# Gated values and attention keys and values as one product of 512 columns, with a new table of delays, in a two-layer hybrid decoder trunk

## The chip, the cores and the metric

The kernel runs on one core of a Trainium2 chip. The core's engines work side by side: TensorE (PE, matrix products), VectorE (DVE), ScalarE (ACT), GpSimd (POOL) and SyncE (SP, which here only issues transfers); 16 DMA engines move data between the large memory outside and the core. Each engine works through its own list in order, and semaphores make one wait for another. The metric is the device time of one execution in microseconds (us).

## What is computed

Two layers over 1024 tokens of 1024 features. In each, one projection of the normalised input is split into three groups of heads, whose gated outputs are put side by side and projected back:

```python
mod = c_act @ w_mod + b_mod
shift, scale, gate = jnp.split(mod[:, None, :], 3, axis=-1)
h = rms_norm(x, pre_gain) * (1.0 + scale) + shift
proj = h @ w_in
(aq, ak, av, ag, rq, rk, rv, rg, gq, gk, gv, gg, ga) = jnp.split(proj, IN_SPLITS, axis=-1)
...
a_out = sliding_window_attention(aq, ak, av, sinks) * jax.nn.silu(ag)
...
r_out = rms_norm(r).reshape(B, S, RET_W) * jax.nn.silu(rg)
...
g = gated_linear_attention(gq..., gk..., gv..., log_a)
g_out = rms_norm(g, gla_norm_gain).reshape(B, S, GLA_W) * jax.nn.silu(gg)
y = jnp.concatenate([a_out, r_out, g_out], axis=-1) @ w_out
return x + gate * rms_norm(y, post_gain)
```

The columns that matter here are `gv` (256: values of the gated linear attention, GLA), and `ak` and `av` (128 each: keys and values of the windowed attention, called kv in the kernel).

## The kernel before

**Products.** Every large product is done in a split form: an operand is a high and a low part in the fp32r type, and three passes (high·high, low·high, high·low) over eight slices of 128 features make 24 matmuls for a tile of 128 tokens. `accum` (L577) issues them. `project` (L586) makes 256 columns of one weight, `project_2` (L599) makes 512 columns out of two weights at once (already used for rk and rv), and `project_T` makes a transposed product. Results land in PSUM, in eight banks of 512 columns: three are called `mm` and hold the projections, five are called `aux` and hold all smaller products.

**Order.** The order of PE's instructions is written by the program itself, since the trunk is recorded under `manual_schedule` for PE; the other engines' instructions are put in order by the framework. The main line issues projections. Everything else is a generator, called a job: it issues some instructions, then yields a delay, or the name of a flag that it needs, and goes on once a clock kept by the program has passed that time. The clock `clk` adds a fixed cost for every matmul that is issued (`mult`, L169). `pump` (called every 7 matmuls of 256 columns or every 4 of 512) lets jobs go on that are due. So a delay decides how many projection matmuls stand on PE between a job's steps; it is no wait on the chip. The delays are the table `L`, read by `lat(key, l)`, which takes the entry `key@1` in layer 1 where there is one. Names in it: `gc1` to `gc6` are the GLA core, `mod1` to `mod6` the modulation, `pre1` the pre-norm, `fin1` and `lay1` the end of a layer, `kv1` and `kv2` the attention keys, `gl1` the GLA gate.

**Input stage of a layer.** After gates (gg, rg) and retention (rq, rk, rv), the projections of gq and gk (`do_gqk`, four of 512 columns), gv (`do_gv`, eight tiles of 256) and kv (`do_kv`, eight tiles of 256) follow. Weights come by DMA in pieces, are split by ACT, DVE (L501) and POOL (L501) into high and low parts in an arena, and `load(l, name)` starts that for the next weight.

**GLA core.** After two tiles of gv a job `gla_core` (L1236) is made, four in a layer, two tiles (cores of 128 tokens, index c) in each. DVE prepares decayed queries and keys (L1244, L1245), PE makes 28 small score matmuls per c into four aux banks (L1269, L1275), ACT (L1278) and DVE (L1279) copy them out, and after the delay `gc3` the next c follows. Then PE multiplies with the running state `stG` (L1291), and DVE updates the state (L1300, L1301); the delay `gc5` sets when the next tile may use it. On DVE also stands the modulation of the next layer: L318 multiplies a piece of modulation weights (buffer `ms`, three buffers) as soon as it has landed, 60 times in all, and L642 normalises in `pre` (L630's function), the first step of the next layer.

**The last product.** In the last layer, `last_output` adds partial results: ACT copies a bank into `kept` (L1518), DVE adds (L1522), ACT squares (L1526).

The lines that carry the three passes:

```python
for a, b in PASSES:
    for k in ks:
        mult(dst, lhs_of(a, k), rhs_of(b, k), q == 0 and ks[0] == 0, ...)
        q += 1
        if q % (CHUNK if len(dst.shape) == 2 else CHUNK // 2 + 1) == 0:
            pump()
```

Of the kernel before, what the change touches and what calls it, by code (L numbers as in the profile page):

```python
# [22 lines left out]
NP_ = NT // 2  # L23
# [68 lines left out]
def trunk(ctx: ExitStack, tc: tile.TileContext, ins, cst, out):  # L92
# [37 lines left out]
    def mm():  # L130
        return ps.tile([P, 512], F32, tag="mm", name=nm("mm"), bufs=MMB)
# [259 lines left out]
    def tables_T():  # L391

        tbs = []
        for i in range(2):
            yield L["tt1"] if i == 0 else L["tt2"]
            pt = aux()
# [61 lines left out]
    def used(l, name):  # L458
        await_flag(("w", l, name))
        return unit(l, name)  # L460
# [14 lines left out]
    def load(l, name, first=None):  # L475
        if l >= DEPTH:
            return
        src = w_out[l] if name[0] == "o" else w_in[l]
        sv = src[ORDER[name]]

        def issue(kc):
            st = stage().rearrange("p (k n) -> p k n", k=2)
            dma("lw", st, sv[:, 2 * kc:2 * kc + 2, :])
            return (st,)

        def conv(kc, st):
            wt = unit(l, name)
            hi, lo = (wt[:, a, 2 * kc:2 * kc + 2, 0:256] for a in range(2))
            if name[0] == "o" and kc == 3:
                A.activation(hi, st, AF.Copy, scale=gnc[:, l:l + 1])  # L490
                V.scalar_tensor_tensor(lo, st, gnc[:, l:l + 1], f(hi), ALU.mult, ALU.subtract)
            else:
                if first:
                    A.activation(hi, st, AF.Copy)
                else:
                    copy(f"whi{kc}", hi, st)
                if first:
                    e = G if first == "AG" and kc in (1, 2) else V
                else:
                    e = G if name[0] == "o" and kc == 2 else eng(f"wlo{kc}")  # L500
                e.tensor_tensor(lo, st, f(hi), ALU.subtract)  # L501
            if kc == 3:
                if name == "gg" and not first:
                    gt = wt[:, :, :, 256:272]
                    st = t1()
                    sg = st[:, 0:128].rearrange("p (k n) -> p k n", k=KT)
                    nc.sync.dma_start(sg, w_ga[l])
                    A.activation(gt[:, 0], sg, AF.Copy)
                    V.tensor_tensor(gt[:, 1], sg, f(gt[:, 0]), ALU.subtract)
                flag(("w", l, name))  # L510

        if first:
            return Paced(issue, conv)
        for kc in range(KT // 2):
            request(l, 1, lambda kc=kc: issue(kc), lambda st, kc=kc: conv(kc, st))
# [410 lines left out]
    kv = {}  # L926
# [707 lines left out]
    def layer(l):  # L1634
# [39 lines left out]
        for t in range(NT):  # L1674
            pm = mm()
# [25 lines left out]
            if hf and kk:  # L1701
                load(l, "aq0")

        def do_gv(p):
            for t in (2 * p, 2 * p + 1):
                pm = mm()
                project(pm[:, 0:256], l, t, used(l, "gv"))
                vs[t] = t1()
                copy("gv", vs[t], pm[:, 0:256])
                if t % 2:  # L1710
                    job(gla_core(l, p, qks[p], (vs[t - 1], vs[t])))
                pump()
            if p == NP_ - 1:
                load(l, "aq1")

        def do_kv(p):
            if p == 0:
                new_kv()
            for t in (2 * p, 2 * p + 1):
                pk = mm()  # L1720
                project(pk[:, 0:256], l, t, used(l, "kv"))
                job(attn_kv(l, t, pk))
                pump()

        do_gqk(0, 0)
        do_gqk(0, 1)
        do_gv(0)
        do_gqk(1, 0)
        do_gv(1)
        do_gqk(1, 1)  # L1730
        do_gv(2)
        do_kv(0)
        do_gv(3)
        for p in range(1, NP_):
            do_kv(p)
        load(l, "ag0")
        job(attn_run(l))
        mx = {}
# [108 lines left out]
L = {"tt6": 5.81, "sw1": 0.0, "ld1": 1.44, "ld2": 1.76, "ld1@1": 1.47, "ld2@1": 1.28, "swW00": 7.11, "swT1": 0.0, "swW11": 1.11, "swW10": 5.83, "tt1": 18.44, "tt2": 2.17, "tt3": 0.28, "tt4": 6.38, "rq1": 14.03, "pf3": 2.74, "pf4@2": 4.29, "pf4@3": 6.52, "pf5": 0.72, "mod1": 2.49, "mod2": 2.57, "mod3": 8.78, "mod4": 9.72, "mod5": 2.35, "mod6": 9.18, "pre1": 4.11, "kv1": 4.46, "kv2": 4.0, "aq1": 5.98, "aq7": 6.05, "ag1": 3.7, "aq2": 2.37, "aq6": 4.8, "aq3": 10.37, "aq4": 6.89, "aq5": 4.91, "hn1": 8.92, "hn2": 2.9, "gz1": 15.13, "gz2": 13.15, "gl1": 2.41, "gd3": 16.85, "gc1": 0.0, "gc2": 1.89, "gc3": 2.35, "gc4": 0.0, "gc6": 0.0, "gc5": 0.87, "rc1": 3.27, "rc2": 3.14, "rc3": 6.62, "rc4": 6.04, "fin1": 6.53, "lay1": 3.11, "gc4@1": 0.0, "mod2@1": 3.98, "mod3@1": 12.28, "mod5@1": 3.22, "mod6@1": 5.73, "pre1@1": 8.15, "kv1@1": 2.99, "kv2@1": 9.56, "aq1@1": 4.93, "aq7@1": 5.06, "ag1@1": 5.28, "aq2@1": 0.6, "aq6@1": 6.29, "aq3@1": 8.77, "aq4@1": 5.59, "aq5@1": 6.76, "hn1@1": 8.25, "hn2@1": 4.04, "gz1@1": 11.89, "gz2@1": 15.8, "gl1@1": 7.44, "gd3@1": 14.88, "gc1@1": 0.0, "gc2@1": 2.13, "gc3@1": 2.18, "gc6@1": 0.63, "gc5@1": 0.0, "rc1@1": 3.65, "rc2@1": 3.04, "rc3@1": 5.19, "rc4@1": 2.96, "fin1@1": 8.92, "lay1@1": 6.35, "mod4@1": 6.36, "mod1@1": 6.19}  # L1847
CHUNK = 7
LAG = 2
VDB = 8  # L1850
# [42 lines left out]
```

## Time and profile before

| | |
|---|---|
| runs, us | 971.81, 974.76, 977.96 (median 974.76) |
| profiled execution, us | 980.54 |
| its span, us | 978.8 |
| instructions | 18540 |
| mean granted clock of PE | 0.991 |
| PE matmuls | 6660 |

The span is the time from the first to the last instruction in the profiled execution; its own time of 980.54 us holds what lies around the span too, and stands 5.8 us over the median of the three runs. The table of the span in 40 slices shows when the engines and the DMA engines are busy:

```profile
PE   8999999999999999999999999999999999999996
DVE  7586777868657858656585464766765477776885
PEclk9999999999999999999999999999999999999999
DMA  9755533503434437668553221351232334487783
```

Each digit is a tenth of a slice of 24.5 us: PE is at 90% or more nearly throughout, DVE moves between 40% and 80%, and the granted clock rounds to full in each slice, so that short stretches at a lower clock are seen only in smaller windows.

### The profile page before, as it was taken

The numbers are of one execution on the slowest core, as the hardware profiler recorded it, in microseconds if no ns is written. First come the engines' busy times: TensorE is split into PE (matmuls) and PEld (weight loads), VectorE is DVE, ScalarE is ACT, GpSimd is POOL, SyncE is SP. The second block draws the span as 40 slices with busy tenths as digits, with TensorE's granted clock in tenths as the row PEclk, the third lists the DMA queues.
The fourth block names the chain that finished last, engine by engine and source line by source line (L and its number), as shares of the span: only waits on it lengthen the run. The fifth ranks groups of instructions, "written<-read, shape, count | busy, mean of one in ns | idle before, by whom it ended". The sixth has DMA issues, their size and how long they took to land. (4 is left out here: it accounts for less than half of the span.)

```text
span 978.8 us, 18540 instructions
## 1 busy us (share of the span) xinstructions
PE 958.3 (98%) x6660; PEld 801.4 (82%) x6660; DVE 668.9 (68%) x1578; ACT 410.8 (42%) x1144; POOL 243.4 (25%) x307
## 2 busy tenths in 40 slices
PE   8999999999999999999999999999999999999996
PEld 6898788889887777778899988888999877777785
DVE  7586777868657858656585464766765477776885
ACT  5665402333323665614454460133333266564231
POOL 3231012323210325411032111122321034545000
PEclk9999999999999999999999999999999999999999
DMA  9755533503434437668553221351232334487783
GB/s 354 294 186 160 173 119 97 178 29 118 153 108 141 114 103 232 204 214 291 178 174 120 94 67 35 119 151 45 88 93 84 98 96 124 144 270 239 253 279 122
DMA packets 107527, 150.26 MB, mean 154 GB/s; under 512 B 11142, under 2 KB 58536, under 8 KB 106412
## 3 DMA queue, kind: packets, MB, share of 16 engines
q1 hardware_dynamic: 96140, 134.75, 43.6%
q10 hardware_dynamic: 11296, 14.34, 4.1%
q8 instruction: 52, 0.85, 0.4%
q14 instruction: 39, 0.32, 0.1%
HBM read 110.25 MB, written 36.70 MB: 150 GB/s over the span
## 5 line engine op out<-in xcount | busy, mean ns | idle before, releaser
L170 PE MATMUL mm<-arena,arena 128*128 128x512 f32 (+2 forms) x1536 | 296.0, 346 | 0.0
L170 PE MATMUL mm<-arena 128*128 128x512 f32 (+2 forms) x1440 | 280.9, 348 | 0.0
L170 PEld LDWEIGHTS mm<-arena,arena 128*128 128x128 f32 x1536 | 238.1, 191 | 33.1 <-issue 1.2
L170 PEld LDWEIGHTS mm<-arena 128*128 128x128 f32 x1440 | 224.2, 190 | 32.9 <-issue 1.5
L170 PE MATMUL mm<-arena,mx 128*128 128x512 f32 (+1 forms) x564 | 132.1, 391 | 2.3 <-ACT kept L1518 2.3
L612 POOL TENSOR_TENSOR sm<-sm,mhalf 128x1 f32<-128x1 f32 (+1 forms) x64 | 58.6, 915 | 300.6 <-DVE sm L609 176.7
L170 PEld LDWEIGHTS mm<-arena,mx 128*128 128x128 f32 x564 | 102.8, 190 | 27.2 <-ACT kept L1518 2.8
L154 ACT ACTIVATE t<-aux 128x256 f32<-128x256 f32 (+2 forms) x124 | 51.4, 434 | 74.9 <-PE aux L185 47.6
L1087 POOL TENSOR_TENSOR smx<-smx,sm 128x512 f32<-128x512 f32 x32 | 36.3, 1134 | 152.2 <-DVE sm L1086 112.0
L1083 ACT ACTIVATE smx<-smx,sm 128x129 f32<-128x129 f32 x128 | 49.9, 392 | 55.7 <-DVE sm L1080 55.7
L154 ACT ACTIVATE arena<-st 128x512 fp32r<-128x512 f32 x94 | 56.2, 627 | 39.7 <-PE mm L170 15.7
L501 POOL TENSOR_TENSOR arena<-st,arena 128x512 fp32r<-128x512 f32 x28 | 41.0, 1466 | 119.4 <-ACT arena L154 101.3
L501 DVE TENSOR_TENSOR arena<-st,arena 128x512 fp32r<-128x512 f32 x80 | 61.7, 796 | 4.9 <-PE mm L170 3.6
L1131 ACT ACTIVATE t<-aux 128x256 f32<-128x256 f32 x32 | 12.2, 382 | 99.2 <-PE aux L170 92.3
L318 DVE SCALAR_TENSOR_TENSOR acc<-ms,c_act,acc 128x512 f32<-128x512 f32 x60 | 45.5, 758 | 9.6 <-DMA ms<-in_w_mod_dram 8.1
L170 PEld LDWEIGHTS aux<-t,mx 32*128 32x128 f32 (+1 forms) x896 | 39.5, 187 | 3.8 <-issue 2.1
L170 PE MATMUL aux<-t,mx 32*128 32x32 f32 (+1 forms) x896 | 40.6, 272 | 0.0
L1425 DVE SCALAR_TENSOR_TENSOR t<-t,sm,t 128x512 f32<-128x512 f32 x32 | 24.1, 780 | 23.8 <-DMA t<-in_x_dram 16.9
L185 PE MATMUL aux<-c_early,t 128*128 128x128 f32 x186 | 33.4, 275 | 2.8 <-DVE t L1124 1.0
L1136 DVE TENSOR_TENSOR t<-aux,sm 128x256 f32<-128x256 f32 x32 | 13.6, 425 | 31.0 <-POOL sm L612 31.0
L1078 DVE COPY_PREDICATED smx<-c_masks,aux 128x256 f32<-128x256 int32 x64 | 25.2, 447 | 13.7 <-ACT smx L154 10.3
L170 PEld LDWEIGHTS aux<-kT,mx 64*128 64x128 f32 x384 | 24.5, 185 | 9.9 <-issue 6.7
(264 smaller groups left out, 1435.4 us busy)
## 6 DMA issues: line engine op xcount, KB each, us to landing
st<-in_w_in_dram SPq DMA_DIRECT2D x96, 256.0 KB, 3.9
ms<-in_w_mod_dram SPq DMA_DIRECT2D x64, 256.0 KB, 3.5
mx<-mixS SPq DMA_DIRECT2D x20, 512.0 KB, 5.1
st<-in_w_last_dram SPq DMA_DIRECT2D x36, 256.0 KB, 3.2
wm<-in_w_m_dram SPq DMA_DIRECT2D x8, 1024.0 KB, 15.8
mixS<-t SPq DMA_DIRECT2D x40, 128.0 KB, 2.8
t<-in_x_dram SPq DMA_DIRECT2D x18, 256.0 KB, 4.8
mixS<-t ACTq DMA_DIRECT2D x32, 128.0 KB, 2.0
```

The costliest lines, as they stand in the source:

```text
L154: A.activation(dst, src, AF.Copy)
L170: T.matmul(dst, lhsT, rhs, start=start, stop=stop)
L185: T.transpose(dst, src, idn)
L318: V.scalar_tensor_tensor(acc, wt, c_act[:, k:k + 1], acc, ALU.mult, ALU.add)
L501: e.tensor_tensor(lo, st, f(hi), ALU.subtract)
L612: G.tensor_tensor(r, r, mhalf[:, :w], ALU.pow)
L1078: V.copy_predicated(sv, curmask.unsqueeze(1).to_broadcast((P, 2, P)), pv[:, :, n // P - 1, :])
L1083: A.activation(sm[:, h, :], sm[:, h, :], AF.Exp, bias=mx[:, h:h + 1], accum_out=sums[:, h:h + 1])
L1087: eng("pn").tensor_tensor(sm[:, :, 0:128], sm[:, :, 0:128], rs.unsqueeze(2).to_broadcast((P, 4, P)), ALU.mult)
L1131: A.activation(sq, po, AF.Square)
L1136: V.tensor_tensor(h4(g1), h4(po), r.unsqueeze(2).to_broadcast((P, 4, 64)), ALU.mult)
L1425: V.scalar_tensor_tensor(xt[j], yg[j], r, xt[j], ALU.mult, ALU.add)
```

## The change

`do_gv` and `do_kv` become one function, `do_gvkv`: each tile is one `project_2` of 512 columns, gv in the lower half of the bank and kv in the upper. The order of the products becomes gqk(0,0), gqk(0,1), gvkv(0), gqk(1,0), gqk(1,1), gvkv(1), gvkv(2), gvkv(3). The load of aq1 moves behind the last of them; the buffers for keys are made at the first. All delays in `L` are set anew.

```diff
-        def do_gv(p):
+        def do_gvkv(p):
+            if p == 0:
+                new_kv()
             for t in (2 * p, 2 * p + 1):
                 pm = mm()
-                project(pm[:, 0:256], l, t, used(l, "gv"))
+                project_2(pm, l, t, used(l, "gv"), used(l, "kv"))
                 vs[t] = t1()
                 copy("gv", vs[t], pm[:, 0:256])
                 if t % 2:
                     job(gla_core(l, p, qks[p], (vs[t - 1], vs[t])))
-                pump()
-            if p == NP_ - 1:
-                load(l, "aq1")
-
-        def do_kv(p):
-            if p == 0:
-                new_kv()
-            for t in (2 * p, 2 * p + 1):
-                pk = mm()
-                project(pk[:, 0:256], l, t, used(l, "kv"))
-                job(attn_kv(l, t, pk))
+                job(attn_kv(l, t, pm[:, 256:512]))
                 pump()
 
         do_gqk(0, 0)
         do_gqk(0, 1)
-        do_gv(0)
+        do_gvkv(0)
         do_gqk(1, 0)
-        do_gv(1)
         do_gqk(1, 1)
-        do_gv(2)
-        do_kv(0)
-        do_gv(3)
         for p in range(1, NP_):
-            do_kv(p)
+            do_gvkv(p)
+        load(l, "aq1")
         load(l, "ag0")
...
-L = {"tt6": 5.81, ... "mod1": 2.49, "mod2": 2.57, ... "pre1": 4.11, ... "gc5": 0.87, ... "fin1": 6.53, "lay1": 3.11, ... "gc3@1": 2.18, ...}
+L = {"tt6": 10.91, ... "mod1": 12.02, "mod2": 2.2, ... "pre1": 11.53, ... "gc5": 1.4, ... "fin1": 8.81, "lay1": 0.0, ... "gc3@1": 0.83, ...}
```

What the new order is at three places, each row an instruction, its line, output and inputs, size and how many in a row.

PE, layer 1, second GLA core, before. The rows of 128x32 are the first of each c's score matmuls (28 of them, cut here), `mm_8091` is a projection, and `stG` the state:

```order
L170 MATMUL mm_8091<-arena_71 128x512 x12
L185 MATMUL aux_8104<-c_early,mx_7527 128x128 x2
L170 MATMUL aux_8109<-t_1487_8051,mx_7527 128x32
...
L185 MATMUL aux_8149<-c_early,t_1476_7991 128x128 x2
L170 MATMUL mm_8091<-arena_71 128x512 x12
L185 MATMUL aux_8170<-c_early,t_1485_8029 128x128 x2
L170 MATMUL aux_8179<-t_1487_8051,mx_7527 128x32
...
L170 MATMUL mm_8221<-arena_483,arena_71 128x256 x21
L170 MATMUL aux_8245<-stG,t_1489_8062 128x256
```

The same place in the changed kernel:

```order
L170 MATMUL mm_7998<-arena_483,arena_71 128x512 x8
L185 MATMUL aux_8015<-c_early,mx_7296 128x128 x2
L170 MATMUL aux_8020<-t_1503_7949,mx_7296 128x32
...
L170 MATMUL mm_7998<-arena_483,arena_71 128x512 x4
L170 MATMUL aux_8064<-t_1503_7949,mx_7296 128x32
...
L185 MATMUL aux_8104<-c_early,t_1513_7989 128x128
L170 MATMUL mm_7998<-arena_483,arena_71 128x512 x4
L170 MATMUL aux_8112<-stG,t_1505_7960 128x256
```

Between the two groups of scores stand four projection matmuls of 512 columns instead of twelve, and behind the second group four of 512 instead of 21 of 256.

DVE at the same place, before: what stands ahead of the copies of the first group out of PSUM (L1279):

```order
L1217 TENSOR_TENSOR t_1493_8067<-mid_8073,t_1491_8065 128x256
L1279 COPY_PREDICATED mx_7529<-c_masks,aux_8109 128x128
L1279 COPY_PREDICATED mx_7529<-c_masks,aux_8110 128x128
L1279 COPY_PREDICATED mx_7529<-c_masks,aux_8111 128x128
L1279 COPY_PREDICATED mx_7529<-c_masks,aux_8112 128x128
L1124 TENSOR_TENSOR t_1506_8153<-aux_8149,t_1505_8152 128x256
```

And in the changed kernel:

```order
L998 TENSOR_TENSOR kT_7524<-aux_8003,kT_7523 128x128
L1244 TENSOR_TENSOR t_1550_8208<-t_1476_7796,t_1508_7964 128x512
L1245 TENSOR_TENSOR t_1551_8209<-t_1476_7796,t_1509_7965 128x512
L1254 TENSOR_TENSOR mx_7296<-t_1550_8208,gs_7978 128x256
L1206 SCALAR_TENSOR_TENSOR t_1555_8223<-c_late,t_1239_6683 128x256
L1279 COPY_PREDICATED mx_7298<-c_masks,aux_8020 128x128
L1279 COPY_PREDICATED mx_7298<-c_masks,aux_8021 128x128
```

Four operations that belong to the next core now stand between the keys' split (L998) and the copies.

DVE in layer 0, third GLA core, before: the state's update (L1301) behind the next layer's modulation (L318):

```order
L318 SCALAR_TENSOR_TENSOR acc_3104<-ms_3432,c_act,acc_3104 128x512
L318 SCALAR_TENSOR_TENSOR acc_3104<-ms_3502,c_act,acc_3104 128x512
L998 TENSOR_TENSOR kT_2859<-aux_3127,kT_2858 128x128
L156 CAST arena_483<-st_3211 128x512
L318 SCALAR_TENSOR_TENSOR acc_3104<-ms_3564,c_act,acc_3104 128x512
L1300 SCALAR_TENSOR_TENSOR stC<-stC,gs_2604,aux_3144 128x64
L1133 TENSOR_REDUCE sm_3158<-t_565_3156 128x4
L1301 TENSOR_TENSOR stG<-stC,c_late 128x256
```

The third core in the changed kernel:

```order
L501 TENSOR_TENSOR arena_483<-st_3392,arena_483 128x512
L1124 TENSOR_TENSOR t_596_3204<-aux_3200,t_595_3203 128x256
L1300 SCALAR_TENSOR_TENSOR stC<-stC,gs_2728,aux_3231 128x64
L998 TENSOR_TENSOR kT_2204<-aux_3238,kT_2203 128x128
L1301 TENSOR_TENSOR stG<-stC,c_late 128x256
```

No L318 stands there any more. On PE, ten matmuls of 256 columns stood between this core's two uses of `stG`, and eight of 512 stand there now. In the last output, ACT's L1518 now stands ahead of the L1526 that it stood behind before.

More of the change, by code (lines that the diff above doesn't have):

```diff
@@ L1846 @@
 EN = {"shw0": "V", "shw1": "A", "shw2": "A", "shw3": "A", "slw0": "V", "slw1": "G", "slw2": "V", "slw3": "G", "sht2": "A", "sht3": "A", "sht4": "A", "slt2": "V", "slt3": "G", "slt4": "G", "sd": "V", "mh0": "A", "mh1": "A", "mh2": "A", "mh3": "A", "mf": "A", "ms0": "V", "ms1": "V", "ms2": "V", "ms3": "V", "yg0": "V", "yg1": "V", "ml0": "V", "ml1": "V", "ml2": "V", "ml3": "V", "mod0": "A", "mod1": "V", "qst": "S", "smh": "A", "sml": "S", "sm0": "S", "sm1": "S", "lao": "S", "sao": "S", "lmix": "S", "ssg": "S", "lsg": "S", "ssr": "S", "lsr": "S", "lx": "S", "sx": "A", "lw": "S", "lwm": "S", "whi0": "V", "whi1": "A", "whi2": "A", "whi3": "A", "wlo0": "V", "wlo1": "V", "wlo2": "V", "wlo3": "G", "xn0": "V", "xn1": "V", "hlo0": "V", "hlo1": "V", "rot0": "V", "rot1": "V", "rdec": "V", "kslo": "V", "qslo": "V", "vlo": "G", "kT": "A", "qT": "A", "sprev": "A", "pn": "G", "pf0": "A", "aoc": "A", "hng": "V", "mh": "A", "gso": "V", "mg": "V", "mgl": "V", "rT": "A", "rv": "A", "gv": "A", "gk": "A", "ak0": "V", "ak1": "V", "ak2": "V", "ak3": "V", "kd0": "G", "kd1": "G", "kd2": "G", "kx1": "G", "kx2": "G", "kx3": "V", "kx4": "V", "qb": "G", "stx": "V"}
-L = {"tt6": 5.81, "sw1": 0.0, "ld1": 1.44, "ld2": 1.76, "ld1@1": 1.47, "ld2@1": 1.28, "swW00": 7.11, "swT1": 0.0, "swW11": 1.11, "swW10": 5.83, "tt1": 18.44, "tt2": 2.17, "tt3": 0.28, "tt4": 6.38, "rq1": 14.03, "pf3": 2.74, "pf4@2": 4.29, "pf4@3": 6.52, "pf5": 0.72, "mod1": 2.49, "mod2": 2.57, "mod3": 8.78, "mod4": 9.72, "mod5": 2.35, "mod6": 9.18, "pre1": 4.11, "kv1": 4.46, "kv2": 4.0, "aq1": 5.98, "aq7": 6.05, "ag1": 3.7, "aq2": 2.37, "aq6": 4.8, "aq3": 10.37, "aq4": 6.89, "aq5": 4.91, "hn1": 8.92, "hn2": 2.9, "gz1": 15.13, "gz2": 13.15, "gl1": 2.41, "gd3": 16.85, "gc1": 0.0, "gc2": 1.89, "gc3": 2.35, "gc4": 0.0, "gc6": 0.0, "gc5": 0.87, "rc1": 3.27, "rc2": 3.14, "rc3": 6.62, "rc4": 6.04, "fin1": 6.53, "lay1": 3.11, "gc4@1": 0.0, "mod2@1": 3.98, "mod3@1": 12.28, "mod5@1": 3.22, "mod6@1": 5.73, "pre1@1": 8.15, "kv1@1": 2.99, "kv2@1": 9.56, "aq1@1": 4.93, "aq7@1": 5.06, "ag1@1": 5.28, "aq2@1": 0.6, "aq6@1": 6.29, "aq3@1": 8.77, "aq4@1": 5.59, "aq5@1": 6.76, "hn1@1": 8.25, "hn2@1": 4.04, "gz1@1": 11.89, "gz2@1": 15.8, "gl1@1": 7.44, "gd3@1": 14.88, "gc1@1": 0.0, "gc2@1": 2.13, "gc3@1": 2.18, "gc6@1": 0.63, "gc5@1": 0.0, "rc1@1": 3.65, "rc2@1": 3.04, "rc3@1": 5.19, "rc4@1": 2.96, "fin1@1": 8.92, "lay1@1": 6.35, "mod4@1": 6.36, "mod1@1": 6.19}
@@ new lines @@
+L = {"tt6": 10.91, "sw1": 1.62, "ld1": 1.66, "ld2": 1.76, "ld1@1": 0.47, "ld2@1": 0.0, "swW00": 5.09, "swT1": 0.43, "swW11": 1.75, "swW10": 6.29, "tt1": 15.2, "tt2": 5.14, "tt3": 7.18, "tt4": 2.39, "rq1": 17.87, "pf3": 2.89, "pf4@2": 4.62, "pf4@3": 6.77, "pf5": 0.72, "mod1": 12.02, "mod2": 2.2, "mod3": 8.51, "mod4": 8.1, "mod5": 4.17, "mod6": 9.91, "pre1": 11.53, "kv1": 4.05, "kv2": 10.66, "aq1": 6.02, "aq7": 6.2, "ag1": 5.04, "aq2": 2.37, "aq6": 6.48, "aq3": 11.06, "aq4": 6.77, "aq5": 4.68, "hn1": 8.92, "hn2": 7.95, "gz1": 18.13, "gz2": 13.12, "gl1": 9.02, "gd3": 17.03, "gc1": 0.98, "gc2": 6.16, "gc3": 1.97, "gc4": 0.1, "gc6": 0.85, "gc5": 1.4, "rc1": 3.56, "rc2": 3.25, "rc3": 7.08, "rc4": 5.77, "fin1": 8.81, "lay1": 0.0, "gc4@1": 0.0, "mod2@1": 3.98, "mod3@1": 12.43, "mod5@1": 4.09, "mod6@1": 7.04, "pre1@1": 7.57, "kv1@1": 5.87, "kv2@1": 2.89, "aq1@1": 4.85, "aq7@1": 5.14, "ag1@1": 2.87, "aq2@1": 0.47, "aq6@1": 6.78, "aq3@1": 8.64, "aq4@1": 5.47, "aq5@1": 5.83, "hn1@1": 8.25, "hn2@1": 1.35, "gz1@1": 15.9, "gz2@1": 11.75, "gl1@1": 4.16, "gd3@1": 16.09, "gc1@1": 0.0, "gc2@1": 2.01, "gc3@1": 0.83, "gc6@1": 1.54, "gc5@1": 0.72, "rc1@1": 4.88, "rc2@1": 2.79, "rc3@1": 5.12, "rc4@1": 1.23, "fin1@1": 6.41, "lay1@1": 12.76, "mod4@1": 6.81, "mod1@1": 6.02}
```

## Prediction

> **What bounds the kernel now.** I read the busy shares first, then what ended TensorE's (PE's) waits, then the granted clock behind each wait, and last the timeline at the places that the change touches. The page's first part (engine, busy us, share of the span, instructions):
>
> ```profile
> PE 958.3 (98%) x6660; PEld 801.4 (82%) x6660; DVE 668.9 (68%) x1578; ACT 410.8 (42%) x1144; POOL 243.4 (25%) x307
> ```
>
> PE is busy for 958.3 of 978.8 us. A change can gain only by taking work or waits from PE, or lose by adding waits. The view of waits, for PE (waiting engine, who ended it, total us, times, longest), without the start-up:
>
> ```profile
> PE mm L170 <- ACT kept L1518: 2.3, 1, 2.3
> PE aux L170 <- DVE sm L609: 1.8, 1, 1.8
> PE aux L185 <- DVE t L1124: 1.0, 1, 1.0
> PE aux L185 <- DVE t L642: 1.0, 1, 1.0
> PE aux L185 <- ACT t L1263: 0.8, 2, 0.6
> ```
>
> They sum to 6.9 us. Behind each (in the order: L609's, L642's, L1263's first, L1124's, L1518's) I took a window and read the granted clock, the number behind the busy times:
>
> ```profile
> 254.00:258.00 4.00, 4.00 (x27) 3.91 (x28) 3.54 (x8) 0.38 (x1) 2.24 (x3) 0.57 0.60 186
> 518.00:522.00 4.00, 4.00 (x34) 4.00 (x34) 3.39 (x7) 3.57 (x11) 2.62 (x6) 1.00 0.28 94
> 674.00:678.00 4.00, 4.00 (x21) 2.90 (x20) 1.08 (x3) 0.33 (x2) 0.00 (x0) 0.57 0.39 131
> 738.80:742.40 3.60, 3.60 (x20) 3.60 (x19) 1.20 (x8) 0.12 (x1) 0.46 (x1) 0.53 0.26 77
> 916.30:919.80 3.50, 3.50 (x9) 2.72 (x10) 2.89 (x7) 0.72 (x2) 0.24 (x1) 0.51 0.60 168
> ```
>
> Four of the five waits are followed by a stretch at a clock of 0.51 to 0.57: (1 − 0.57) × 4.00 = 1.72 us of work lost, or (1 − 0.51) × 3.50 = 1.72. So a short wait costs itself and then about 1.7 us; only the second window (1.00) shows none. Waits and dips together are 6.9 + 4 × 1.7 = 13.7 us. That is all that better delays can win.
>
> **The merge.** 768 products of 256 columns (8 tiles × 24, for gated values and for attention's keys and values, in two layers) become 384 of 512. Multiply-adds stay the same, so what is saved is what a matmul costs beyond its columns. From start to start, on PE's timeline (start, us, count at the end), two stretches of each kind with the row that follows:
>
> ```profile
> 899.68 5.76 PE L170 MATMUL aux<-arena,mx 128*128 128x512 f32 x24
> 905.28 1.10 PE L170 MATMUL mm<-arena,mx 128*128 128x512 f32 x4
> ...
> 775.57 5.78 PE L170 MATMUL mm<-arena 128*128 128x512 f32 x24
> 781.28 0.98 PE L170 MATMUL aux<-kT,mx 64*128 64x256 f32 x12
> ...
> 546.93 8.34 PE L170 MATMUL mm<-arena,arena 128*128 128x256 f32 x69
> 555.11 0.40 PE L170 MATMUL aux<-gaT,gwt 128*128 128x512 f32 x1
> ...
> 274.85 5.65 PE L170 MATMUL mm<-arena 128*128 128x256 f32 x45
> 280.33 0.27 PE L185 MATMUL aux<-c_early,t 128*128 128x128 f32 x1
> ```
>
> 512 columns: 5.60 / 24 = 233.3 ns and 5.71 / 24 = 237.9 ns. 256 columns: 8.18 / 69 = 118.6 ns and 5.48 / 45 = 121.8 ns. A pair of 256 against one of 512 is then worth 2 × 118.6 − 237.9 = −0.7 ns at the least and 2 × 121.8 − 233.3 = 10.3 ns at the most; × 384 that is −0.3 to 4.0 us. I take the two stretches in which nothing else is mixed and the count is highest for their kind: 237.2 − 233.3 = 3.9 ns × 384 = **−1.5 us**. The Trainium skill, TensorE: Matmul & The Clock Gate, section "Wait — 56ns, not 53.3ns?", says that a warm matmul costs its columns plus a fixed 2.5 ns or so; by that the merge would give 384 × 2.5 = 1.0 us in place of my 1.5, as an estimate from that page. The rows stand between. Copies out of the bank (ACT's copy of gv, attention's rotary from the upper half) read the same columns as before: 0.
>
> **Weights.** The merged product needs kv's weights together with gv's, where before gv's ran first. In layer 1 the last conversion of these weights and the first product that reads them were:
>
> ```profile
> 651.67 1.69 POOL L501 TENSOR_TENSOR arena<-st,arena 128x512 fp32r<-128x512 f32 x1 [4.64 <-ACT arena L154]
> 659.42 2.67 PE L170 MATMUL mm<-arena 128*128 128x256 f32 x21
> ```
>
> It ended at 653.36, with 6.1 us to spare. Cost 0; what hides it is the gq/gk product ahead, and if the weights came over 6 us later, the wait would start there. Moving the load of aq1 behind the last product delays a transfer whose reader comes one projection and more later: 0.
>
> **The new delays, layer 0's GLA.** The longest mid-run wait of PE in layer 0:
>
> ```profile
> 249.25 1.46 PE L170 MATMUL mm<-arena 128*128 128x256 f32 x10
> 250.74 0.75 DVE L318 SCALAR_TENSOR_TENSOR acc<-ms,c_act,acc 128x512 f32<-128x512 f32 x1 [1.30 <-DMA ms<-in_w_mod_dram]
> 251.93 0.42 DVE L1301 TENSOR_TENSOR stG<-stC,c_late 128x256 f32<-128x256 f32 x1
> 252.49 0.67 PE L170 MATMUL aux<-stG,t 128*128 128x256 f32 x2 [1.78 <-DVE sm L609]
> ```
>
> VectorE (DVE) works in order. A transfer of modulation weights landed late, L318 waited 1.30 us for it, and the state update L1301 that PE needs stood behind L318. Only ten matmuls of 256 (1.46 us) lay between PE's two uses of the state. Now eight products of 512 lie there: 8 × 233.3 = 1.87 us, 0.4 us more, and, by the order of DVE, no L318 stands near the state updates of this core at all; two stand ahead of each update of the first core, where the same could happen (mod2, the delay from such a load to L318, even falls from 2.57 to 2.20). Between the wait kept whole at the new place (0) and gone with its dip (1.78 + 1.72 = 3.5), I take it as gone in this execution: **−3.5**.
>
> **Layer 0 to layer 1.** The chain of finish and the next pre-norm let PE wait once, with no dip behind it:
>
> ```profile
> 516.89 1.09 PE L185 MATMUL aux<-c_early,t 128*128 128x128 f32 x8 [0.95 <-DVE t L642]
> ```
>
> fin1 and pre1 grow by 2.3 and 7.4 us, lay1 shrinks by 3.1: more room in sum. From 0 to 0.95; since the rows moved elsewhere may be late in their turn, I take half: **−0.5**.
>
> **Layer 1's GLA.** A core computes two groups of scores (28 small matmuls each into four aux banks), and the second group needs the banks that the first one holds until ACT (L1278) and DVE (L1279) have copied them out. Before, this looked so:
>
> ```profile
> 692.71 0.40 PE L170 MATMUL aux<-t 32*128 32x32 f32 x8
> 693.13 0.68 ACT L1278 ACTIVATE mx<-aux 128x96 f32<-128x96 f32 x4 [0.18 <-PE aux L170]
> 693.41 0.89 DVE L1279 COPY_PREDICATED mx<-c_masks,aux 128x128 f32<-128x128 int32 x4 [1.48 <-ACT mx L1278]
> 693.24 3.04 PE L170 MATMUL mm<-arena 128*128 128x512 f32 x12
> 696.42 0.85 PE L170 MATMUL aux<-t,mx 32*128 32x32 f32 x21
> ```
>
> The group ended at 693.11; the copies were done at 694.30, 1.2 us later; PE filled 3.04 us with twelve products of 512. With gc3 of layer 1 at 0.83 in place of 2.18, only four stand there: 4 × 233.3 = 0.93 us. The first of the four DVE copies frees its bank at about 0.3 + 0.89 / 4 = 0.5 us, the last at 1.2, and the group takes banks one after the other, with one spare; so a wait of about 0.3 us remains where DVE is prompt. In the second core DVE is not: four operations now stand ahead of L1279, by the groups of lines (us in all, mean ns):
>
> ```profile
> L1244 DVE TENSOR_TENSOR t<-t,t 128x512 f32<-128x512 f32 x8 | 6.3, 785 | 0.0
> L1245 DVE TENSOR_TENSOR t<-t,t 128x512 f32<-128x512 f32 x8 | 7.0, 876 | 4.8 <-PE aux L170 3.5 <-issue 1.3
> ...
> L1254 DVE TENSOR_TENSOR mx<-t,gs 128x256 f32<-128x256 f32 x8 | 4.2, 529 | 0.1
> ```
>
> The larger three make 2.2 us; those that started before the group's end only count in part, so I take 0.7 to 1.0 in two of the cores and 0.3 in the other two, about 2.0 us in all, with two dips: 2.0 + 3.4 = 5.4. Before, the waits of L1263 and L1124 with two dips were 1.8 + 3.4 = 5.2. **+0.2**, from −5.2 (none of either) to +8.8 (the fourth rival).
>
> **The end.** In the last output ACT did this ahead of PE's last wait:
>
> ```profile
> 914.90 0.63 ACT L1526 ACTIVATE st<-t 128x512 f32<-128x512 f32 x1 [0.24 <-DVE t L1522]
> 915.52 0.58 ACT L1518 ACTIVATE kept<-mm 128x512 f32<-128x512 f32 x1
> 916.16 1.07 PE L170 MATMUL mm<-arena,mx 128*128 128x512 f32 x2 [2.31 <-ACT kept L1518]
> ```
>
> Now L1518 stands ahead of L1526: the wait becomes 2.31 − 0.63 = 1.7, the dip stays: **−0.6** (0 if L1518 waits for something else, −4.0 if wait and dip go).
>
> **The sum** against the profiled execution (980.5 us, span 978.8): −1.5 − 3.5 − 0.5 + 0.2 − 0.6 = −5.9. The median of the runs shown, 974.8, is 5.8 under it. A late transfer is the kind of thing that differs between executions, so I assume that half of the 3.5 isn't in the median run: −5.9 + 1.75 = −4.15, and 974.8 − 4.15 = **970.6**.
>
> **Rivals.**
> 1. All mid-run waits go: the merge and 1.75 as above, the whole 0.95, layer 1's 5.2 and the end's 0.6: 974.8 − 10.05 = 964.7. For it: every one is short, and the new delays are longer at nearly all places with a wait. Against it: gc3 of layer 1 was shortened.
> 2. Nothing is gained on balance: the merge at its lower bound, each wait gone replaced by one elsewhere: about 974.8 + 0.3 = 975. For it: PE is 98% busy, and delays only trade room in one place for room in another.
> 3. The weights of kv come late. Against it stands the 6.1 us; if they were 2 us beyond it, 2 + 1.7 in one layer: 970.6 + 3.7 = 974.3, held in with the second.
> 4. Slower: layer 1's second groups wait in all four cores. It decides where DVE's L1279 starts over 0.5 us behind the group's end. Price: 1.2 us for the first bank, 0.6 at the state update behind it (four products now lie there too), 1.7 for the dip: 4 × 3.5 = 14.0 against 5.2, +8.8: 974.8 − 4.15 − 0.2 + 8.8 = 979.2. For it: 0.93 us is under the 1.2 measured for prompt copies. Against: one bank is spare. It needs the dips: TensorE: Matmul & The Clock Gate of the Trainium skill, in its table of efficiency rules and in Part 1, wants an idle window of some 3.4 us before the clock is halved. By that rule none of these waits would cost more than itself: the 3.5 of layer 0 would be 1.8 and the sum would end at 971.5 in place of 970.6, and the fourth case 4 × 1.8 − 1.8 = 5.4 over it, an estimate from that page. The four windows above, behind waits of 0.6 to 2.3 us, disagree, so I keep the dips.
>
> **How the numbers follow.** Forecast 0.45 (its own range 966 to 975), all waits gone 0.20, nothing gained 0.18, layer 1 throttled 0.17. The range, 962.5 to 979.5, leaves out about half of the fourth and a quarter of the first rival. A measurement here tells apart about 1%, 9.7 us: faster is below 965.0, slower above 984.5. Faster takes most of the first rival and a little of the forecast: 0.20. Slower takes the upper end of the fourth: 0.06. Same: 0.74.
>
> **What would show it.** The merge: 384 fewer PE matmuls, and starts 233 ns apart in gated values. Layer 0: no PE wait ended by L609 or L1301 and no clock under 0.6 behind the third GLA core. Layer 1: PE waits of 0.3 to 1.0 us ended by L1278 or L1279, with dips behind two. The end: PE's wait for L1518 near 1.7 us. The forecast is wrong if layer 1's GLA loses more than 10 us, or if a wait for weights appears ahead of the first merged product.

## The result, and the profile after

| | before | changed |
|---|---|---|
| median of 20 runs, us | 976.84 (971.81 to 979.81) | 973.32 (970.11 to 975.65) |
| ratio to before | 1 | 0.9968, 95% interval 0.9957 to 0.9980 |
| profiled execution: time, us | 980.54 | 971.85 |
| its span, us | 978.8 | 969.9 |
| PE matmuls | 6660 | 6276 |

The changed kernel is 0.3% faster, 3.1 us by the ratio, in the middle of the predicted range (970.6, from 962.5 to 979.5) and within 1%. The median of before over 20 runs is 976.8, 2 us over that of the three runs known at the time of the prediction. The two profiled executions differ by 8.7 us, far more than the medians: the first profile of before was slower than all of its 20 timed runs. So what is read from that pair has to be checked on second profiles. In the experiments below, runs more than 1.5% above the fastest of their kernel are left out; only the kernel "apart, new delays" had such runs, two of six at 1007 us.

The first part of the page of the changed kernel, and its view of PE's waits (us in all, times, longest), answer to those of before:

```profile
span 969.9 us, 17774 instructions
PE 953.0 (98%) x6276; PEld 779.5 (80%) x6276; DVE 664.1 (68%) x1578; ACT 410.9 (42%) x1144; POOL 240.7 (25%) x307
```

```profile
PE mm L170 <- DVE t L1522: 1.5, 1, 1.5
PE aux L185 <- ACT t L1263: 1.5, 1, 1.5
...
PE aux L170 <- DVE t L1136: 0.3, 1, 0.3
PE mm L170 <- DMA a<-mixS: 0.3, 1, 0.3
```

PE is busy for 5.3 us less. Of the five waits of before, those of layer 0 (L609), of the pre-norm (L642) and of L1124 are gone, that of L1518 is now one for L1522, and that of L1263 has nearly doubled. The windows behind the last two (us, then the busy times of PE, PEld, DVE, ACT and POOL, then granted clock, DMA share and GB/s):

```profile
737.33:740.74 3.41, 2.79 (x61) 2.25 (x59) 2.31 (x9) 1.26 (x2) 0.30 (x1) 1.00 0.82 217
740.74:744.16 3.42, 2.45 (x10) 1.61 (x10) 1.49 (x6) 2.12 (x8) 1.27 (x1) 0.50 0.97 303
744.16:747.57 3.41, 3.41 (x58) 3.35 (x59) 0.03 (x1) 0.31 (x3) 0.00 (x0) 0.50 0.59 182
747.57:750.98 3.41, 3.41 (x13) 2.84 (x11) 1.06 (x5) 0.54 (x4) 0.00 (x0) 0.50 0.70 228
925.06:928.47 3.41, 1.94 (x9) 1.22 (x7) 3.31 (x6) 0.73 (x3) 0.00 (x0) 1.00 0.86 245
928.47:931.88 3.41, 3.36 (x15) 2.76 (x16) 1.90 (x5) 1.21 (x3) 0.55 (x1) 1.00 0.98 314
```

In layer 1's last GLA core the clock is halved for 10.24 us at a stretch, three times what any wait of before brought. PE is busy for 2.45 + 3.41 + 3.41 us of it, so that up to half of that, 4.6 us, is lost. At the end, a wait of the same length is followed by no dip at all.

What made PE wait in that core, on the timeline of ACT and PE:

```profile
739.55 0.63 ACT L154 ACTIVATE arena<-st 128x512 fp32r<-128x512 f32 x1 [0.57 <-DMA st<-in_w_in_dram]
740.75 0.63 ACT L154 ACTIVATE arena<-st 128x512 fp32r<-128x512 f32 x1 [0.57 <-DMA st<-in_w_in_dram]
741.29 0.37 ACT L1263 ACTIVATE t<-aux 128x256 f32<-128x256 f32 x1
741.55 0.67 ACT L1278 ACTIVATE mx<-aux 128x96 f32<-128x96 f32 x4
741.71 0.69 PE L185 MATMUL aux<-c_early,t 128*128 128x128 f32 x2 [1.49 <-ACT t L1263]
```

ACT converts weight pieces that land about 1.2 us apart, waits 0.57 us for each, and the small copy L1263, whose bank PE needs, stands behind them. The place that the prediction watched instead, the second score group of a core, looks like this in the first core of layer 1:

```profile
671.11 0.40 PE L170 MATMUL aux<-t 32*128 32x32 f32 x8
671.44 1.20 PE L170 MATMUL mm<-arena 128*128 128x512 f32 x4
672.57 1.20 PE L170 MATMUL aux<-t,mx 32*128 32x32 f32 x35
```

Four products, then at once the next group: no wait.

### The profile page after: what moved, and what is told of

Read it like the earlier page. It is cut to its first block, busy times and chain, and to the rows that moved or that the text cites. A ratio compares the mean times of both kernels' runs of the same rounds, so it can differ in the third digit from the quotient of the medians.

```text
span 969.9 us, 17774 instructions
## 1 busy us (share of the span) xinstructions
PE 953.0 (98%) x6276; PEld 779.5 (80%) x6276; DVE 664.1 (68%) x1578; ACT 410.9 (42%) x1144; POOL 240.7 (25%) x307
## 5 line engine op out<-in xcount | busy, mean ns | idle before, releaser
L170 PE MATMUL mm<-arena 128*128 128x512 f32 (+2 forms) x1248 | 276.8, 374 | 0.0
L170 PEld LDWEIGHTS mm<-arena,arena 128*128 128x128 f32 x1344 | 223.3, 189 | 41.2 <-issue 2.8
L170 PEld LDWEIGHTS mm<-arena 128*128 128x128 f32 x1248 | 211.0, 189 | 40.7 <-issue 3.2
L501 POOL TENSOR_TENSOR arena<-st,arena 128x512 fp32r<-128x512 f32 x28 | 43.1, 1541 | 101.9 <-ACT arena L154 61.1
L501 DVE TENSOR_TENSOR arena<-st,arena 128x512 fp32r<-128x512 f32 x80 | 64.4, 829 | 5.8 <-ACT arena L154 4.0
L318 DVE SCALAR_TENSOR_TENSOR acc<-ms,c_act,acc 128x512 f32<-128x512 f32 x60 | 45.1, 751 | 9.1 <-DMA ms<-in_w_mod_dram 8.5
L170 PEld LDWEIGHTS aux<-t,mx 32*128 32x128 f32 (+1 forms) x896 | 42.5, 195 | 6.2 <-issue 2.8
L170 PE MATMUL aux<-t,mx 32*128 32x32 f32 (+1 forms) x896 | 43.5, 280 | 0.4 <-DVE t L1136 0.3
L185 PE MATMUL aux<-c_early,t 128*128 128x128 f32 (+1 forms) x186 | 34.2, 278 | 1.5 <-ACT t L1263 1.5
L1136 DVE TENSOR_TENSOR t<-aux,sm 128x256 f32<-128x256 f32 x32 | 13.6, 425 | 29.0 <-POOL sm L612 29.0
```

Source lines behind the costliest of these rows:

```text
L170: T.matmul(dst, lhsT, rhs, start=start, stop=stop)
L185: T.transpose(dst, src, idn)
L318: V.scalar_tensor_tensor(acc, wt, c_act[:, k:k + 1], acc, ALU.mult, ALU.add)
L1136: V.tensor_tensor(h4(g1), h4(po), r.unsqueeze(2).to_broadcast((P, 4, 64)), ALU.mult)
```

## The experiments

Each ratio is to before as timed on the same chip in the same hours, in three groups of runs: the first holds the four rows below before, the second gc3 back, loader back and before with the new gc3, the third the rest. The mean granted clock of each run, listed with its time, turned out to be worth reading beside the times: with a span of some 970 us, 0.001 of mean clock is up to 0.97 us of work lost. It is a coarse measure: the one profile with no dip at all (gc3 back, again) shows 0.997, and so do two with one dip of 3.41 us.

| kernel | median, us | ratio to before (95% interval) | mean clock of its runs |
|---|---|---|---|
| before (three groups of runs) | 976.2, 977.6, 977.0 | 1 | 0.9952, 0.9941, 0.9945 |
| changed, again | 973.07 | 0.9970 (0.9956 to 0.9983) | 0.9925 |
| two halves | 985.38 | 1.0083 (1.0053 to 1.0113) | 0.9867 |
| merged, old delays | 983.33 | 1.0072 (1.0049 to 1.0096) | 0.9922 |
| apart, new delays | 994.76 | 1.0187 (1.0157 to 1.0217) | 0.9825 |
| gc3 back | 969.03 | 0.9915 (0.9892 to 0.9938) | 0.9960 |
| gc3 back, again | 969.04 | 0.9919 (0.9902 to 0.9936) | 0.9953 |
| loader back | 971.84 | 0.9947 (0.9930 to 0.9964) | 0.9926 |
| before with the new gc3 | 985.71 | 1.0101 (1.0061 to 1.0141) | 0.9877 |
| two halves, gc3 back | 974.59 | 0.9976 (0.9955 to 0.9996) | 0.9933 |
| gc3 longer | 990.25 | 1.0146 (1.0124 to 1.0168) | 0.9866 |
| gc3 and loader back | 968.27 | 0.9912 (0.9894 to 0.9929) | 0.9967 |

**The changed kernel once more.**

> The changed kernel once more, for comparison on the same chip. Expected: 3 to 4 us under before, with two to four windows at half clock in the profile. If the wait of 1.49 us ended by L1263 in layer 1 (with 10.24 us at half clock) belongs to the order and not to that one execution, it is there again; if it is an accident of one late transfer, it is gone and another wait may stand elsewhere.

It measured the same again, and its profile has the wait for L1263 (1.87 us) and the 10.24 us at half clock at the same place: they belong to the order. A fourth window at half clock stands in layer 0's third core (at 261.52 us), where the first profile has none. Against before on the same chip, its mean clock is lower by 0.0027, up to 2.6 us of work that the faster kernel gives back.

**The kernel before once more**, for its profile only.

> The kernel before once more, for a second profile. If its first profile was a bad execution, this one has one or two windows at half clock in place of four, and PE's wait of 1.78 us in layer 0's third GLA core, behind a late transfer, is gone; if those belong to the order, they are there again.

Of its waits, by the view of PE's waits:

```profile
PE mm L170 <- DMA a<-mixS: 1.5, 1, 1.5
PE mm L170 <- ACT kept L1518: 1.2, 1, 1.2
PE aux L185 <- DVE t L642: 1.0, 1, 1.0
PE aux L185 <- ACT t L1263: 0.9, 2, 0.7
...
PE aux L185 <- DVE t L1124: 0.5, 1, 0.5
```

The wait of 1.78 us for L609 in layer 0 isn't there, so it doesn't belong to the order. The mean clock of that first profile was 0.991, where the 52 runs of before timed beside the experiments have 0.9946 in the mean, so it also had more half clock than most. The wait for L642 is there, as in every kernel with the old delays. The clock is halved twice in this profile, for 3.41 us each: at 734.62 us in layer 1's last core, where the stretch ahead holds the wait for L1124, and behind this window in layer 0's third core:

```profile
236.28:239.69 3.41, 3.37 (x71) 3.10 (x69) 3.41 (x15) 2.09 (x8) 0.00 (x0) 1.00 0.01 2
239.69:243.10 3.41, 3.41 (x18) 3.41 (x17) 2.65 (x12) 0.88 (x3) 0.46 (x1) 0.50 0.45 144
```

PE is busy for 3.37 of 3.41 us there. No wait stands ahead of the dip at 239.69. PE's timeline shows what the window holds:

```profile
236.43 1.54 PE L170 MATMUL aux<-t,mx 32*128 32x32 f32 x48
237.79 0.40 PE L170 MATMUL aux<-t 32*128 32x32 f32 x8
238.12 1.05 PE L170 MATMUL aux<-c_late,acc 128*128 128x1 f32 x8
```

It is a score group, whose matmuls take 32 columns and use 32 of the 128 rows, then eight products of a single column, and little else. Here busy is not the same as streaming.

**One part alone, and the other part alone.** The delay table of before in the changed kernel, and the new table in the kernel before:

```diff
 # changed kernel
-L = {... "mod1": 12.02, ... "gc3@1": 0.83, ...}
+L = {... "mod1": 2.49, ... "gc3@1": 2.18, ...}
 # kernel before
-L = {... "mod1": 2.49, ... "gc3@1": 2.18, ...}
+L = {... "mod1": 12.02, ... "gc3@1": 0.83, ...}
```

> The merged product with the delays of before. Theory 1, merge and delays add up: 1.5 us or more under before. Rival, the delays of before fit only the old order of products: at 256-column steps the clock stood elsewhere, waits of 0.5 to 2 us appear at several places, and the time is 0 to 10 us over before.

> Gated values and keys and values apart as before, with the new delays. Theory 1, the delays alone are worth what is left of the gain after the merge: 1 to 3 us under before. Rival, the new delays fit only the merged order: slower than before by 0 to 10 us, through new waits of PE in the GLA of either layer.

The merge alone is 7 us slower than before, the delays alone 18 us by the ratio, both together 3 us faster. The rival was right in kind both times, though the second loss is beyond the 10 us that it allowed: either table fits its own order of products and not the other. With the old table PE waits 4.3 us for L1279, the longest time in layer 1's last core; with the new table and products apart, 6.7 us for L1124, most of it in layer 1, and 2.3 us for L1136 in layer 0:

```profile
PE aux L185 <- DVE mx L1279: 4.3, 3, 2.9
```

```profile
PE aux L170 <- DVE t L1124: 6.7, 3, 4.6
...
PE aux L170 <- DVE t L1136: 2.3, 1, 2.3
```

Waits are not all of it. The mean clock of these runs, 0.9922 and 0.9825 against 0.9952, stands for up to 3 of the 7 us and up to 12 of the 18: in the profile with products apart, each of these waits over 1 us is followed by 6.8 or 10.2 us at half clock, 23.9 us in all.

**The merge alone, delays and steps kept.** Each product of 512 columns as two of 256, with a pump at the same points:

```diff
-                project_2(pm, l, t, used(l, "gv"), used(l, "kv"))
+                await_flag(("hT", l, t))
+                halves(pm, l, t, used(l, "gv"), used(l, "kv"))
...
+    def halves(pm, l, t, w0, w1):
+        c = slice((t % 2) * P, (t % 2) * P + P)
+        h = hT[(l, t // 2)]
+        q = 0
+        for i, w in enumerate((w0, w1)):
+            for a, b in PASSES:
+                for k in range(KT):
+                    mult(pm[:, 256 * i:256 * i + 256], h[:, a, k, c], w[:, b, k, 0:256], q % 24 == 0, q % 24 == 23)
+                    q += 1
+                    if q % 8 == 0:
+                        pump()
```

> The changed kernel with each product of 512 columns made as two of 256, first gv's 24 matmuls and then kv's, all delays kept, steps of the jobs at the same places on PE. Theory 1, the merge saves what a matmul costs beyond its columns: slower than the changed kernel by 1.5 us as the prediction's rows said (range 0 to 4), with 384 matmuls more. Rival, the merge saves nothing on PE and the delays are all of the gain: equal within 0.5 us.

> The same with each product of 512 columns made as two of 256. Here the two score groups stand apart, so the half clock should take less of the difference: if the merge is worth what the profiles leave after idle time and half clock are taken off, it is 3 to 4 us slower than the kernel with gc3 put back; if the prediction's rows were right, 1.5 us; if waits that the other engines' shifted order brings are most of the 12 us seen without gc3 put back, over 6 us.

The second has gc3 of layer 1 at 2.18 besides, as in an experiment further below. The first is 12 us slower than the changed kernel, far from either expectation, and its clock can account for half: 0.9867 against 0.9925 is up to 5.6 us. The order of DVE and ACT also shifts in a few dozen places, and its profile waits 2.4 us in layer 1 for the line that is L1124 in the changed kernel (L1136 here, with twelve lines added). The second, with less half clock about, is 5.6 us over its reference, between what was expected for the merge and for shifted waits, and its runs fall in two groups: seven at a mean clock of 0.995 or more (971.2 to 974.9 us) and five at 0.991 or less (977.6 to 979.7). So only like runs can show the merge: two at 0.997 took 971.2 and 971.4, two of the reference at 0.997 took 968.2 and 968.3. That is 3.0 us for 384 matmuls saved, 7.8 ns each, from few runs.

Like mean clock is not like work, though: the profile of the run of 971.2 us has one dip and its reference none. So I also took from PE's busy time, in each profile, half of what falls into the windows at half clock (about 1.7 us for each of 3.41). That leaves 953.4 − 1.7 = 951.7 here and 949.6 in the reference, 958.3 − 6.8 = 951.5 before and 953.0 − 4.6 = 948.4 changed, so 2.1 and 3.1 us; the second profiles of before and changed give 951.4 and 948.6. The start-up differs as well. The record of the clock begins at 7 to 9 us; in the first profile of before the same matmul of 128 columns starts every 213 ns ahead of that point and every 112 ns behind it. PE's busy time ahead of it is 4.0 us here and 5.8 us in the reference. With half of that taken off too, the merge is worth 3.0 us in this pair (949.7 against 946.7) and 3.1 us between two halves and changed (949.7 against 946.6).

```profile
PE 953.4 (98%) x6660; PEld 798.7 (82%) x6660; DVE 665.3 (69%) x1578; ACT 410.1 (42%) x1144; POOL 241.0 (25%) x307
```

```profile
PE 949.6 (98%) x6276; PEld 776.1 (80%) x6276; DVE 665.1 (69%) x1578; ACT 410.7 (42%) x1144; POOL 239.9 (25%) x307
```

**One delay, both ways.** gc3 of layer 1 sets how many products stand between a core's two score groups, four in the changed kernel, twelve before:

```diff
 # changed kernel
-"gc3@1": 0.83
+"gc3@1": 2.18
 # kernel before
-"gc3@1": 2.18
+"gc3@1": 0.83
```

> The changed kernel with one delay put back, gc3 of layer 1 from 0.83 to 2.18, so that more projection products stand between the two score groups of a layer 1 core. Theory A, a stretch of 3.41 us that holds the small score matmuls and little else is followed by 3.41 us at half clock, and the change pushed the two groups of a core into one such stretch: the mean clock rises from about 0.992 to 0.995, the time falls by 2 to 4 us under the changed kernel. Rival B, the half clock in layer 1 follows only PE's wait for L1263 in the last core, a late weight transfer: that wait of 1.5 to 1.9 us and 10.24 us at half clock stand there again, and the time is within 1 us of the changed kernel.

> The kernel before with one delay changed, gc3 of layer 1 from 2.18 to 0.83. Theory A: more windows at half clock in layer 1, mean clock from 0.995 to 0.993 or lower, 2 to 6 us over before. Rival B: no such windows without late weights, within 1 us of before.

> The changed kernel with gc3 of layer 1 at 2.18 once more, as the reference of this call and to confirm it: 8 us under before (ratio 0.990 to 0.994), mean clock 0.995 to 0.997.

Times and mean clocks moved as theory A said, in both directions. Put back, the delay makes the changed kernel 4 us faster, 8 us under before, and the repeat confirms it; the mean clock rises from 0.9925 to 0.996. In the kernel before, the new value costs 8 to 10 us and lowers the clock from 0.994 to 0.988.

The traces show another mechanism than two groups in one stretch. In the changed kernel, PE's timeline of the last core of layer 1 is this (the grid of the clock has its borders at 737.33, 740.74, 744.16 and 747.57):

```profile
737.96 1.92 PE L170 MATMUL aux<-t,mx 32*128 32x32 f32 x47
...
741.71 0.69 PE L185 MATMUL aux<-c_early,t 128*128 128x128 f32 x2 [1.49 <-ACT t L1263]
742.05 2.06 PE L170 MATMUL mm<-arena,arena 128*128 128x512 f32 x4
744.03 2.79 PE L170 MATMUL aux<-t,mx 32*128 32x32 f32 x48
```

The first group and the first 0.5 us of the wait make the stretch that is followed by half clock. The rest of the wait makes the next stretch thin as well, and the second group, four products on, falls into the third, at half clock already. So the dips are three in a row and not one. In the first three cores the same four products stand between the groups, without a wait, and no dip follows. The windows of the reference run at the same place:

```profile
737.40:740.80 3.40, 2.62 (x56) 2.17 (x54) 2.50 (x9) 2.14 (x6) 1.97 (x2) 1.00 0.67 192
740.80:744.20 3.40, 3.40 (x31) 2.84 (x28) 3.33 (x11) 1.57 (x8) 1.29 (x1) 1.00 0.67 199
744.20:747.60 3.40, 3.40 (x65) 2.84 (x64) 2.40 (x9) 1.23 (x6) 0.00 (x0) 1.00 0.57 198
```

Here twelve products of 512 columns follow the first group. The wait for L1263 is gone too, and 0.78 us for L1136 stands in its place, so not all of the 4 us is the clock: at a mean clock of 0.995 runs of the two kernels still lie 1.4 to 2.0 us apart (971.4 us for the changed kernel, 969.4 to 969.9 with gc3 back). Spacing and wait weren't separated further.

In the kernel before with the new gc3, the profile is of its fastest run (982.3 us, 0.993). It has one dip in layer 1's GLA, no more than the second profile of before, and not behind two crowded groups: the first group of the third core waits for a bank.

```profile
712.30 1.41 PE L170 MATMUL aux<-t,mx 32*128 32x32 f32 x41 [3.09 <-DVE t L1124]
```

```profile
710.55:713.96 3.41, 1.66 (x50) 1.63 (x50) 2.63 (x7) 1.51 (x4) 0.00 (x0) 1.00 0.41 120
713.96:717.38 3.42, 3.42 (x25) 3.18 (x28) 1.81 (x9) 1.53 (x7) 0.00 (x0) 0.50 0.72 228
```

So the dip came without the late weight that rival B held to be needed, but in this execution not without a wait. What its four slower runs lose, at a mean clock of 0.980 to 0.989, no profile shows.

**The weight loader's delays**, alone and with gc3, and **gc3 longer still**:

```diff
-"ld1@1": 0.47, "ld2@1": 0.0
+"ld1@1": 1.47, "ld2@1": 1.28
```

> The changed kernel with layer 1's delays of the weight loader put back, ld1 from 0.47 to 1.47 and ld2 from 0 to 1.28. Theory B, ACT stands at a conversion of a weight piece whose transfer has not landed, and L1263, for which PE waits, stands behind it: with room for the transfer the wait of 1.5 to 1.9 us goes, with it the half clock of 10.24 us (5.1 us), and the time falls by 3 to 6 us under the changed kernel. Rival A, the score matmuls alone lower the clock: the wait may go, but windows at half clock stay in layer 1's GLA, and the time falls by less than 2 us. Third, later conversions are themselves too late for the next product: slower by 1 us or more.

> gc3 of layer 1 at 2.18 and layer 1's loader delays at 1.47 and 1.28, both as before. The loader's delays alone gave 1.2 us or less. If both gains are apart from each other: 0.5 to 1.5 us under gc3 alone. If the loader's delays mattered only through the crowded score groups: the same within 1 us.

```diff
-"gc3@1": 0.83
+"gc3@1": 3.2
```

> gc3 of layer 1 at 3.2, about 16 projection products between the two score groups in place of 12. Theory A, once no stretch of 3.41 us falls under about 0.3 of full matmul streaming there is nothing more to win: within 1 us of gc3 at 2.18. Rival: the more products, the better (1 us or more faster), or the second group now comes too late for what follows it (1 us or more slower).

The delays didn't give the transfer the room that theory B counted on: with them back the wait for L1263 stands there still (1.6 us), with 6.83 us at half clock behind it, and the gain of 1 to 2 us lies inside the intervals. Whether the dips would go with the wait is thus not tested by it. With gc3 they give 968.27 against 969.04, which isn't told apart; it is the lowest median of all, 0.9912 of before. Its profile has no wait for L1263, but a dip of 3.41 us behind the first group of the last core all the same (at 741.04), followed by the eight next products and no second dip. So gc3 at 2.18 doesn't always keep the dip away; here it stayed short. With the loader's delays alone, the timeline of ACT shows the same conversions, 1.2 and 1.35 us behind one another and each waiting for its transfer: the transfers set that pace there, and the delay in the plan doesn't.

And 16 products between the groups are 21 us worse than 12, in the direction of the last rival and by far more than it said. The mean clock, 0.9866 against 0.9953, stands for up to 8 of these. PE waits 4.7 us for L1136, nearly all of it within the first groups of layer 1's last two cores, and 7.3 us at the end, and what leads from the one to the other wasn't followed up:

```profile
PE mm L170 <- DVE t L1522: 7.3, 2, 6.5
PE aux L170 <- DVE t L1136: 4.7, 3, 2.4
```

## Why the prediction was right, by its steps

The time was right within 3 us, and the gain, forecast at 4.2 us, was 3.1. That is in part luck: the merge was put 1.5 us too low and layer 1's GLA about 2 us too cheap, and the two cancelled.

- **The merge, −1.5.** The mechanism was right and the size too small: 3.0 us between runs of like clock, 2.1 to 3.1 by PE's busy time, inside the stated bounds of −0.3 to 4.0. Of the four stretches quoted I took the two that gave 3.9 ns for a pair; the like runs give 7.8, between that and the 10.3 of the other end.
- **Weights, 0.** Right: no wait stands ahead of the first merged product in either layer.
- **Layer 0's GLA, −3.5 in that execution, half of it in the median.** The wait is gone, but the second profile of before doesn't have it either. Halving it was right in kind; of the two profiles of before, one had it. The dip was not tied to it: it stands in that core in both profiles of before and in the second of the changed kernel. Waits and dips together fell by 1.4 us in the mean of two profiles each.
- **Layer 0 to 1, −0.5.** The wait of 0.95 us for L642 is gone in both profiles of the changed kernel: −1.0.
- **Layer 1's GLA, +0.2.** This step failed. It put the cost at waits of the second score groups (0.3 to 1.0 us in each core) with a dip behind two of them. No group of the first three cores waited. One wait stands in the last core, for L1263, and the loss is in the clock: 10.24 us at half speed. Waits and half clock of this stage are 5.2 and 3.1 us in the two profiles of before, and 6.2 and 6.5 in those of the changed kernel: +2.2 in the mean. What failed is the rule from the first five windows, that a short wait costs one dip of 1.7 us. The runs show that a dip follows a stretch with little to stream, mostly with a wait in it and sometimes without, and that the next thin stretch prolongs it. gc3, which the prediction named as the danger, is a delay worth setting back, at 4 us in the changed kernel and 8 to 10 in the kernel before, though not by waits of the second groups.
- **The end, −0.6.** In the first pair, 2.31 us and a dip became 1.52 and none. In the second profile of before that wait was 1.18 us with no dip, and 1.5 us for a transfer beside it. It swings from execution to execution by more than was predicted for it; in the mean of two profiles each, 3.4 us became 1.6.

Of the rivals, the first (all waits go; its terms add up to 10.0 us, not 10.05), the second (no gain) and the third (late weights) fell. The fourth, slower through layer 1's GLA, had the place right and not the way: one core lost and not four, 6.2 to 6.5 us where it priced 14.0, and the merge paid for it.

By the two profiles of each kernel, the merge (−3.0), layer 0's GLA (−1.4), the next layer's start (−1.0), layer 1's GLA (+2.2) and the end (−1.8) make −5.0 of the 5.6 us between the mean spans of these profiles. The timed runs differ by 3.1 us, of which the merge leaves next to nothing: there the lower clock, at most +2.6, and fewer waits would have to cancel. How they do in a typical run stays open, since only two profiles of each kernel show waits.

## What to carry to other kernels

In this kernel, delays that were tuned for one order of products held for that order only: each half of the change alone was 7 to 18 us slower, though both together are faster, so a sum of parts says little about a part. Before shortening the distance between groups of small matmuls, look at what each stretch of 3.41 us will hold in columns times rows, and at the waits that fall into it, and not at the waits alone. And read the mean granted clock of every timed run beside its time: it showed that the faster kernel was throttled more, which pointed to the delay that won another 4 us.

## What the runs showed of the hardware

In these runs the clock of PE changes in stretches of 3.41 us on a fixed grid: in the first profile of before, the four dips start at 254.17, 674.01, 738.86 and 916.36 us, and the later three lie 123.0, 142.0 and 194.0 times 3.413 us behind the first. In every other profile with several dips they lie whole multiples apart too. For all fourteen profiles I added up, in each such stretch from 46 us to the end of the matmuls, the columns of all matmuls that start in it, each weighted by the share of the 128 rows that it uses, as a share of what 512-column matmuls at 233.3 ns would stream in it (7490 columns):

```
share of full streaming   stretches   next one at half clock
under 0.20                       22                       22
0.20 to 0.30                     10                       10
0.30 to 0.40                     28                        5
0.40 to 0.50                     86                        1
over 0.50                      3602                        0
```

Under 0.3 the next stretch ran at half clock every time, over 0.4 but once in 3688. Where the grid is laid, and matmul records that may be missing, move single counts a little. The share was chosen with most of these profiles at hand, so the table describes them and tests little. The table also holds stretches that ran at half clock themselves and so could stream half at most: ten of the 32 under 0.3.

Idle time alone doesn't decide it, but it belongs to most dips. In 63 of the stretches at full clock PE was idle for 0.5 us or more; half clock followed all 19 of these with a share of 0.30 or less, and one of the 37 over 0.4. For one, 1.5 us of waiting among dense products (925.06 to 928.47 in the changed kernel) left the clock alone. The other way round, 23 of the 26 dips that began at full clock followed one of the 63; the 3.37 busy us of score matmuls (236.28 in the second profile of before) are one of the three that didn't. The Trainium skill, TensorE: Matmul & The Clock Gate, Part 1, describes a free-running activity window of about this length, which the grid bears out; its table of states gives an idle window of some 3.4 us as what leads to half clock. That the runs contradict, if idle means without matmuls: of the 32 stretches under 0.3, PE was idle throughout in two, and busy for 3.37 us or more in nine, of which two ran at full clock and seven at half.
